# The last piece of a final RMS norm: a GpSimd power in place of ScalarE's inverse root and a Newton step

## The chip, the cores and the metric

The kernel runs on one core of a Trainium2 chip. The metric is the device time of one execution in microseconds (us); before the change the median of three runs is 1436.55 us (1436.22 to 1438.27).

## The reference

The kernel computes one layer of a streaming encoder on 1024 positions of 1024 channels: two convolution mixers with gates, an output projection, a SwiGLU feed-forward part, and at the end an RMS norm. Only the end is touched by the change:

```python
def rms_norm(x, g):
    xf = x.astype(jnp.float32)
    y = xf * lax.rsqrt(jnp.mean(xf * xf, axis=-1, keepdims=True) + EPS)
    return (y * g.astype(jnp.float32)).astype(x.dtype)

x = x + g2 * jnp.einsum('bsf,fd->bsd', jax.nn.silu(a) * bgate, w_ffn_out[l])
return rms_norm(x, final_norm_g)
```

For each position the square of 1024 channels is averaged, EPS = 1e-6 is added, and every channel of the position is multiplied by the inverse square root of the sum (called the factor here) and by its own gain g.

## The kernel before, in words

Channels lie on the 128 partitions, in eight tiles of 128 channels (j = 0 to 7); positions lie along a row of a tile. A factor for 256 positions is therefore a tile of 128 x 256 in which all partitions hold the same numbers: a product of TensorE with a matrix of ones sums over the partitions and writes the sum to each of them.

The last matrix products (the feed-forward part's second weights) are made with the positions cut in three pieces, `PIECES = [(0, 512), (512, 256), (768, 256)]`. For each piece and each j the evacuation from PSUM adds the product to x in place (L1994, VectorE). Then `piece_done` follows: ScalarE squares x with a scale of 1/32, so that the sum is a mean (L1967). For the tiles that GpSimd will scale, ScalarE also multiplies x by the gain (L1973). VectorE adds the squares up (L2017). When the piece has all its squares, `piece_norm` sums them over the partitions on TensorE (L2045, tile `ss` in PSUM), and ScalarE makes a first inverse root of `ss` with EPS as bias (L624, tile `rf`) and half its square (L2047, tile `rq`). `piece_rstd` improves it by a Newton step in two instructions of VectorE (L2054, L2056). They leave the negative of the factor, since the step is written as (t - 1.5) * r. The sign is undone by using `ng`, the negated gains, for the product with the gain.

`piece_scale` multiplies. Of the first two pieces GpSimd multiplies all eight tiles by the factor (L2033). Of the last piece, whose work comes after the last matrix product, GpSimd takes the tiles j = 1, 4 and 7 (`POOL_LAST`), and VectorE the other five, with gain and factor in one instruction (L2035). For this the last piece's factor is held twice: VectorE reads `rf` in PSUM, where the Newton step's second instruction writes it, and GpSimd reads `rp`, a copy in SBUF that ScalarE makes (L2024). SyncE's queue sends the results out as they come: the last two pieces in eight DMAs (L2038) of two tiles each, in the order of j. So the first DMA of the last piece waits for tile 0 of VectorE and tile 1 of GpSimd.

Each engine works through its own list in order, and waits for other engines at semaphores. The lists are set by the order of the code and by hints (`issue_after`); a scheduler places the instructions of the last pieces among those of the matrix products. Before the last piece's root a tiny ScalarE instruction with the same function (L650) is placed by `load_rsqrt`.

Of the kernel before, what the change touches and what calls it, by code (L numbers as in the profile page):

```python
# [35 lines left out]
F32 = mybir.dt.float32  # L36
F32R = mybir.dt.float32r
AF = mybir.ActivationFunctionType
ALU = mybir.AluOpType

P = 128
# [3 lines left out]
KC = D // P  # L45
# [8 lines left out]
V_GMIX, V_GFFN, V_GFIN, V_LNG, V_LNB, V_CB = (8 * i for i in range(6))  # L54
# [60 lines left out]
APART = 3  # L115
# [26 lines left out]
PIECES = [(0, 512), (512, 256), (768, 256)]  # L142
# [7 lines left out]
def block_kernel(ctx: ExitStack, tc: tile.TileContext, x0, xT, c, vecs, ada, w_first, w_plain, w_duals,  # L150
                 w_short, w_conf, w_o, w_fi, w_fo0, w_fo1, outT):
    nc = tc.nc

    def pool(name, bufs, **kw):
        return ctx.enter_context(tc.tile_pool(name=name, bufs=bufs, **kw))
# [10 lines left out]
    cp = pool("const", 1)  # L166
# [13 lines left out]
    def ps_tile(name):  # L180
        return psp.tile([P, H], F32, tag="ps", name=name)

    def ps2_tile(name):
        return ps2p.tile([P, H], F32, tag="ps2", name=name)

    def hl_tile(name, dt=F32R):
        return tp.tile([P, H], dt, tag="t", name=name)
# [7 lines left out]
    def f32(t):  # L195
        return t.bitcast(F32)
# [7 lines left out]
    vec = cp.tile([P, NV], F32, name="vec")  # L204
# [2 lines left out]
    nc.vector.memset(ones, 1.0)  # L207
    ones_c = cp.tile([P, P], F32R, name="ones_c")
    nc.gpsimd.memset(f32(ones_c), 1.0)
    eps1 = cp.tile([P, 1], F32, name="eps1")  # L210
    nc.vector.memset(eps1, EPS)
    eps2 = cp.tile([P, 1], F32, name="eps2")
# [4 lines left out]
    ng = cp.tile([P, V_LNG], F32, name="ng")  # L217
# [402 lines left out]
    def rstd_start(ss, eps, name, n=H, tile_of=g_tile):  # L620

        r, t = tile_of(name + "r")[:, :n], tile_of(name + "t")[:, :n]
        ss = ss[:, :n]
        act = nc.scalar.activation(r, ss, AF.Abs_reciprocal_sqrt, bias=eps)  # L624
        return ss, eps, r, t, act.ins
# [21 lines left out]
    def load_rsqrt(ins):  # L647

        with tc.issue_after(ins):
            act = nc.scalar.activation(cp.tile([P, 1], F32, name="rs"), ones[:, :1], AF.Abs_reciprocal_sqrt)  # L650
        load_rsqrt.ins = act.ins
# [94 lines left out]
    def uc_tile(name, n=T + CK - 1, dt=F32):  # L746
        return ucp.tile([P, T + CK - 1], dt, tag="uc", name=name)[:, :n]
# [30 lines left out]
    for k in range(0, KC, 2):  # L778
        t = uc_tile("x0", T)
# [477 lines left out]
    sqs = [None, None]  # L1257
# [565 lines left out]
    ss = ps_tile("ss")  # L1823
# [108 lines left out]
    for g in range(FINAL):  # L1932
        n = 2 * GROUPS[g] * P
# [20 lines left out]
    LAST = len(PIECES) - 1  # L1954

    def wide_tile(name):
        return hl_tile(name, dt=F32)

    def on_pool(i, j):
        return i < LAST or j in POOL_LAST  # L1960

    def piece_done(i, j):
        nonlocal norm, acc
        at, n = PIECES[i]
        dst = x1[j][:, at : at + n]
        sq = wide_tile("sq")[:, :n]
        act = nc.scalar.activation(sq, dst, AF.Square, scale=1.0 / 32.0)  # L1967
        sqs.append(sq)
        c = len(sqs) - 1
        if i == LAST and c == KC - 1:  # L1970
            load_rsqrt(act.ins)
        if on_pool(i, j):
            nc.scalar.activation(dst, dst, AF.Copy, scale=ng[:, V_GFIN + j : V_GFIN + j + 1])  # L1973
        lag = LAG if i == LAST else 0
        if c > lag and c - lag < KC - APART * (i == LAST):
            piece_sum(i, c - lag)
        if i and c == NORM_AT[i - 1]:
            norm = piece_norm(i - 1, [acc])
        if i and c == RSTD_AT:
            with tc.issue_after(last_evac.ins):  # L1980
                rf = piece_rstd(i - 1, *norm)
            piece_scale(i - 1, rf)
        if c == KC - 1 and i < LAST:
            acc = sqs[0]
            sqs.clear()

    def last_evac(d, i):
        at, n = PIECES[i]

        def evac(p, m, ps):  # L1990
            low = m in "574"
            j = 2 * d + p + 4 * low
            dst = x1[j][:, slice(at, at + n) if i else halves[m in "67"]]
            last_evac.ins = nc.vector.scalar_tensor_tensor(  # L1994
                out=dst, in0=ps, scalar=ng2[:, j : j + 1] if low else modc(40 + j), in1=dst, op0=ALU.mult, op1=ALU.add
            ).ins
            if m in "2453":
                piece_done(i, j)
        return evac

    def piece_product(banks, d, m, i):
        at, n = PIECES[i]
        off = at % H
        apart = (d, m) == (0, "5")
        for p in range(2):
            if m == "5":
                banks[d, p] = ps_tile("z")[:, :n]
            ps = banks[d, p]
            for k in range(KH):
                xs = tuple(t[:, off : off + n] for t in to[FINAL, m][k])  # L2010
                c0 = ((0 if apart else p) * KH + k) * P
                mm3([ps], slice(c0, c0 + P), w5[p] if apart else ws[d, m], [xs], m == "5" and k == 0, k == KH - 1, m == "3")
            last_evac(d, i)(p, m, ps)

    def piece_sum(i, j):
        with tc.issue_after(last_evac.ins):
            nc.vector.tensor_tensor(sqs[0], sqs[0], sqs[j], ALU.add)  # L2017

    def piece_scale(i, rf):
        at, n = PIECES[i]  # L2020
        m = H // n
        if i == LAST:
            rp = wide_tile("rp")[:, :n]
            nc.scalar.copy(rp, rf)  # L2024
        else:
            rp = rf
        for j in range(0, KC, m):
            ys = wide_tile("y") if m > 1 else x1[j][:, at : at + n]
            ys = ys.rearrange("p (m n) -> p m n", n=n)
            for d in range(m):  # L2030
                y, src = ys[:, d], x1[j + d][:, at : at + n]
                if on_pool(i, j + d):
                    nc.gpsimd.tensor_tensor(y, src, rp, ALU.mult)  # L2033
                else:
                    nc.vector.scalar_tensor_tensor(  # L2035
                        out=y, in0=src, scalar=ng[:, V_GFIN + j + d : V_GFIN + j + d + 1], in1=rf, op0=ALU.mult, op1=ALU.mult
                    )
            nc.sync.dma_start(outT[j : j + m, :, at : at + n].rearrange("m p n -> p m n"), ys)  # L2038

    def piece_norm(i, parts):  # L2040

        n = PIECES[i][1]
        ss, r, q = (t[:, :n] for t in (ps_tile("ss"), wide_tile("rf"), wide_tile("rq")))
        for part in parts:
            nc.tensor.matmul(ss, ones, part, start=part is parts[0], stop=part is parts[-1])  # L2045
        rstd_start(ss, eps1, "rf", n, lambda name: r)
        nc.scalar.activation(q, r, AF.Square, scale=0.5 ** 0.5)  # L2047
        return ss, r, q

    def piece_rstd(i, ss, r, q):  # L2050

        n = PIECES[i][1]
        t = ps2_tile("rft")[:, :n]
        nc.vector.scalar_tensor_tensor(out=t, in0=ss, scalar=EPS, in1=q, op0=ALU.add, op1=ALU.mult)  # L2054
        out = ps2_tile("rf")[:, :n] if i == LAST else r
        nc.vector.scalar_tensor_tensor(out=out, in0=t, scalar=1.5, in1=r, op0=ALU.subtract, op1=ALU.mult)  # L2056
        return out

    norm, acc, sqs = None, None, []
    for d in range(2):  # L2060
# [4 lines left out]
    for i in range(1, len(PIECES)):  # L2065
        banks = {}
        for m in "53":
            for d in range(2):
                if i == 1 and (d, m) != (0, "5"):
                    ws[d, m] = next_w()  # L2070
                piece_product(banks, d, m, i)
    piece_scale(LAST, piece_rstd(LAST, *piece_norm(LAST, [sqs[0]] + sqs[KC - APART :])))


def _chunks(v):
# [74 lines left out]
```

## Time and profile before

| | |
|---|---|
| median of three runs | 1436.55 us (1436.22 to 1438.27) |
| the profiled execution's own time | 1434.56 us |
| its span, first to last instruction | 1432.5 us |
| TensorE busy | 1419.0 us, 99% of the span |
| VectorE, ScalarE, GpSimd busy | 1201.2, 663.7, 538.6 us |
| last product of the last piece's sum (L2045) | runs from 1421.75 to 1423.64 us of the span |
| last DMA of results issued | at 1428.3 us |

The times in the timeline and the windows are microseconds from the span's start. TensorE is nearly always busy, so almost the whole span is its work; only the last nine microseconds, behind the last matrix product, belong to the other engines. That is where the change lies. A row of a timeline gives the start, the time that it covers, the engine, the line and operation, the tiles written and read, the shape, how many instructions are merged in the row, and in brackets how long the engine was idle before and what released it.

### The profile page before, as it was taken

To read this page: it belongs to the slowest core of one execution; us is meant where nothing else is said; L and a number is where in the kernel's file an instruction comes from. 1 tells how busy PE (TensorE), PEld (TensorE's weight loads), DVE (VectorE), ACT (ScalarE), POOL (GpSimd) and SP (SyncE) were. 2 spreads that over 40 slices of the span, in tenths; PEclk is the share of its full clock that TensorE was granted. 3 is DMA by queue.
4 is the path that set the end of the run, shared out by engine and by line. 5 is a ranking of instruction groups with operands and counts; after the bars stand their busy time and mean duration, and the time that the engine had idled before them with its cause. 6 is when DMAs were issued, how large, how long until landed. Compare 5 with 4: busy or idle time off the path is not lost.

```text
span 1432.5 us, 17797 instructions
## 1 busy us (share of the span) xinstructions
PE 1419.0 (99%) x6274; PEld 1165.3 (81%) x6274; DVE 1201.2 (84%) x1680; ACT 663.7 (46%) x980; POOL 538.6 (38%) x526
## 2 busy tenths in 40 slices
PE   9999999999999999999999999999999999999997
PEld 5888888888888888878888788888888888888887
DVE  8987998999998999989989987777867665866676
ACT  4873333333333446557454765444444433321235
POOL 0007877777677672012121211111111015653405
PEclk9999999999999999999999999999999999999999
DMA  9775654333337879978797667665454349996903
GB/s 365 273 234 161 192 191 147 103 118 104 124 116 223 225 227 337 261 221 175 229 282 225 164 189 245 211 205 176 155 176 156 127 149 342 385 379 196 348 1 118
DMA packets 103596, 295.50 MB, mean 206 GB/s; under 512 B 11682, under 2 KB 13730, under 8 KB 103507
## 3 DMA queue, kind: packets, MB, share of 16 engines
q1 hardware_dynamic: 51280, 161.50, 33.0%
q0 software_dynamic: 47040, 119.22, 29.9%
q10 hardware_dynamic: 5186, 13.64, 2.4%
q8 instruction: 49, 0.80, 0.2%
q14 instruction: 41, 0.33, 0.1%
HBM read 219.87 MB, written 84.41 MB: 212 GB/s over the span
## 4 chain that ended last, share of the span: by engine, by line
PE 90%; DVE 4%; ACT 1%; POOL 1%; issue 1%; DMA 1%; POOLq 0%; SPq 0%; DVEq 0%; ACTq 0%
PE bank L554 14%; PE bank L556 14%; PE bank L553 14%; PE x L556 8%; PE x L553 8%; PE x L554 8%; PE z L553 4%; PE z L556 4%; PE z L554 4%; PE y L553 2%; PE y L556 2%; PE y L554 2%; PE lead L549 1%; DVE wl L255 1%; POOL x L2033 1%
## 5 line engine op out<-in xcount | busy, mean ns | idle before, releaser
L254 ACT CAST wh<-raw 128x1024 fp32r<-128x1024 f32 (+2 forms) x256 | 265.0, 1037 | 379.1 <-PE bank L554 117.9
L255 DVE TENSOR_TENSOR wl<-raw,wh 128x1024 fp32r<-128x1024 f32 (+2 forms) x178 | 212.8, 1196 | 45.6 <-ACT wh L254 43.7
L255 POOL TENSOR_TENSOR wl<-raw,wh 128x1024 fp32r<-128x1024 f32 x78 | 195.6, 2520 | 71.9 <-ACT wh L254 71.7
L1212 DVE SCALAR_TENSOR_TENSOR c<-diff,vec,c 128x512 f32<-128x512 f32 x232 | 163.4, 748 | 1.5
L1781 POOL DMA_DIRECT2D hid<-stage x70 | 37.4, 534 | 312.5 <-DVE stage L610 301.7
L556 PE MATMUL bank<-th,wl 128*128 128x512 f32 x336 | 130.8, 389 | 0.0
L554 PE MATMUL bank<-tl,wh 128*128 128x512 f32 x336 | 130.7, 389 | 0.0
L553 PE MATMUL bank<-th,wh 128*128 128x512 f32 x336 | 130.7, 389 | 0.0
L556 PEld LDWEIGHTS bank<-th,wl 128*128 128x128 f32 x336 | 63.1, 188 | 13.3 <-POOL wl L255 0.3
L554 PEld LDWEIGHTS bank<-tl,wh 128*128 128x128 f32 x336 | 63.1, 188 | 13.1
L553 PEld LDWEIGHTS bank<-th,wh 128*128 128x128 f32 x336 | 63.1, 188 | 13.0
L553 PE MATMUL x<-th,wh 128*128 128x512 f32 x176 | 68.5, 389 | 0.0
L554 PE MATMUL x<-tl,wh 128*128 128x512 f32 x176 | 68.5, 389 | 0.0
L556 PE MATMUL x<-th,wl 128*128 128x512 f32 x176 | 68.4, 390 | 0.0
L1212 DVE SCALAR_TENSOR_TENSOR c<-u,wsum,c 128x512 f32<-128x512 f32 x96 | 66.8, 749 | 0.8
L610 DVE TENSOR_TENSOR stage<-g,stage 128x512 fp32r<-128x512 f32 x60 | 41.1, 688 | 24.0 <-ACT stage L609 24.0
L609 ACT CAST stage<-g 128x512 fp32r<-128x512 f32 x60 | 37.2, 620 | 51.8 <-DMA hid<-stage 34.9
L1805 POOL DMA_DIRECT2D th<-hid x77 | 41.2, 535 | 50.2 <-PE x L556 23.2
L1805 POOL DMA_DIRECT2D tl<-hid x77 | 41.2, 535 | 19.6 <-DMA tl<-hid 3.8
L553 PE MATMUL bank<-t2h,wh 128*128 128x512 f32 x112 | 43.6, 389 | 0.0
L554 PE MATMUL bank<-t2l,wh 128*128 128x512 f32 x112 | 43.6, 389 | 0.0
L556 PE MATMUL bank<-t2h,wl 128*128 128x512 f32 x112 | 43.6, 389 | 0.0
(794 smaller groups left out, 4117.6 us busy)
## 6 DMA issues: line engine op xcount, KB each, us to landing
hid<-stage POOLq DMA_DIRECT2D x70, 512.0 KB, 4.5
raw<-in_w_duals SPq DMA_DIRECT2D x65, 512.0 KB, 4.5
raw<-in_w_fi SPq DMA_DIRECT2D x45, 512.0 KB, 3.8
th<-hid POOLq DMA_DIRECT2D x77, 256.0 KB, 6.4
tl<-hid POOLq DMA_DIRECT2D x77, 256.0 KB, 6.2
ada<-in_ada SPq DMA_DIRECT2D x34, 512.0 KB, 5.4
raw<-in_w_fo SPq DMA_DIRECT2D x16, 512.0 KB, 6.4
raw<-in_ada SPq DMA_DIRECT2D x14, 512.0 KB, 3.6
```

Of the source, the lines that this page charges most:

```text
L254: hi = nc.scalar.copy(wh, raw)
L255: lo = lo_engine.tensor_tensor(wl, raw, f32(wh), ALU.subtract)
L549: mm3.ins = nc.tensor.matmul(ps, w[0][:, wsl], x, start=first, stop=last, skip_group_check=again).ins
L553: nc.tensor.matmul(ps, wh, xh, start=first, stop=False, skip_group_check=again)
L554: nc.tensor.matmul(ps, wh, xl, start=False, stop=False, skip_group_check=again)
L556: mm3.ins = nc.tensor.matmul(ps, wl, xh, start=False, stop=last, skip_group_check=again).ins
L609: t_split.act = nc.scalar.copy(hi, src).ins
L610: t_split.ins = nc.vector.tensor_tensor(lo, src, f32(hi), ALU.subtract).ins
L1212: tap.ins = nc.vector.scalar_tensor_tensor(out=out, in0=src[:, s : s + H], scalar=wt, in1=acc, op0=ALU.mult, op1=ALU.add).ins
L1781: nc.gpsimd.dma_start(hid_dram[key], s)
L1805: nc.gpsimd.dma_start(t, hid_dram[key][:, s])
L2033: nc.gpsimd.tensor_tensor(y, src, rp, ALU.mult)
```

## The change

A tile `power` of 128 x 256 is added that holds -0.5 everywhere; GpSimd fills it at the start. For the last piece alone, `piece_norm` now copies the mean square plus EPS from PSUM to SBUF on ScalarE (function Identity with EPS as bias, into `rf`), and GpSimd raises each element of it to the power in `power`, in place. `piece_rstd` is not called for this piece, and the tiny ScalarE instruction ahead of its root goes. The factor now is in SBUF first, where GpSimd reads it; ScalarE copies it to PSUM for VectorE. The factor is positive, so the last piece uses the gains `vec` and not the negated `ng`.

```diff
+    power = cp.tile([P, PIECES[-1][1]], F32, name="power")
+    nc.gpsimd.memset(power, -0.5)
...
-        if i == LAST and c == KC - 1:
-            load_rsqrt(act.ins)
         if on_pool(i, j):
-            nc.scalar.activation(dst, dst, AF.Copy, scale=ng[:, V_GFIN + j : V_GFIN + j + 1])
+            nc.scalar.activation(dst, dst, AF.Copy, scale=(vec if i == LAST else ng)[:, V_GFIN + j : V_GFIN + j + 1])
...
         if i == LAST:
-            rp = wide_tile("rp")[:, :n]
-            nc.scalar.copy(rp, rf)
+            rp, rf = rf, ps2_tile("rf")[:, :n]
+            nc.scalar.copy(rf, rp)
...
-                        out=y, in0=src, scalar=ng[:, V_GFIN + j + d : V_GFIN + j + d + 1], in1=rf, op0=ALU.mult, op1=ALU.mult
+                        out=y, in0=src, scalar=vec[:, V_GFIN + j + d : V_GFIN + j + d + 1], in1=rf, op0=ALU.mult, op1=ALU.mult
...
             nc.tensor.matmul(ss, ones, part, start=part is parts[0], stop=part is parts[-1])
+        if i == LAST:
+            nc.scalar.activation(r, ss, AF.Identity, bias=eps1)
+            nc.gpsimd.tensor_tensor(r, r, power, ALU.pow)
+            return r
         rstd_start(ss, eps1, "rf", n, lambda name: r)
...
-        out = ps2_tile("rf")[:, :n] if i == LAST else r
-        nc.vector.scalar_tensor_tensor(out=out, in0=t, scalar=1.5, in1=r, op0=ALU.subtract, op1=ALU.mult)
-        return out
+        nc.vector.scalar_tensor_tensor(out=r, in0=t, scalar=1.5, in1=r, op0=ALU.subtract, op1=ALU.mult)
+        return r
...
-    piece_scale(LAST, piece_rstd(LAST, *piece_norm(LAST, [sqs[0]] + sqs[KC - APART :])))
+    piece_scale(LAST, piece_norm(LAST, [sqs[0]] + sqs[KC - APART :]))
```

The lists of TensorE and SyncE are unchanged. Two more places on the lists matter. First the end of GpSimd's list, before the change: the two last tiles of the middle piece (read with `rf`), then the three tiles of the last piece (read with `rp`).

```order
L2033 TENSOR_TENSOR y<-x_10227,rf 128x256
L2033 TENSOR_TENSOR y<-x_10229,rf 128x256
L2033 TENSOR_TENSOR y<-x_9747,rp 128x256
L2033 TENSOR_TENSOR y<-x_9748,rp 128x256
L2033 TENSOR_TENSOR y<-x_10229,rp 128x256
```

And the same place with the change, where the waits at semaphores stand behind the rows:

```order
L2033 TENSOR_TENSOR y<-x_10229,rf 128x256 [waits PE_49]
L2033 TENSOR_TENSOR y<-x_10231,rf 128x256
L2048 TENSOR_TENSOR rf<-rf,power 128x256 [waits Activation_49]
L2033 TENSOR_TENSOR y<-x_9749,rf 128x256 [waits PE_49,Pool_49]
L2033 TENSOR_TENSOR y<-x_9750,rf 128x256 [waits DMASW2_49,PE_49]
L2033 TENSOR_TENSOR y<-x_10231,rf 128x256 [waits DMASW1_49,PE_49]
```

The power stands behind the whole middle piece and in front of the last piece's three tiles, the first of which waits for GpSimd's own semaphore (Pool_49).

Second the end of ScalarE's list, before the change: the last squares, then the small instruction (`rs`), the root, half its square and the copy.

```order
L1967 ACTIVATE sq<-x_9750 128x256
L1967 ACTIVATE sq<-x_10225 128x256
L650 ACTIVATE rs<-ones 128x1
L624 ACTIVATE rf<-ss,eps_101 128x256
L2047 ACTIVATE rq<-rf 128x256
L2024 COPY rp<-rf 128x256
```

With the change two instructions follow the squares, and the second waits for GpSimd:

```order
L1969 ACTIVATE sq<-x_9752 128x256 [waits DMASW3_49,DVE_49]
L1969 ACTIVATE sq<-x_10227 128x256 [waits DMASW6_49,DVE_49]
L2047 ACTIVATE rf<-ss,eps_103 128x256 [waits DMASW5_49,PE_49]
L2024 COPY rf<-rf 128x256 [waits Pool_49]
L2148 UNCONDITIONAL_BRANCH
```

On VectorE the two Newton instructions (L2054 and L2056) are gone from the end of the list; its five products (L2035) come straight behind the last evacuation, and now wait for ScalarE's copy.

## The prediction

> **What bounds the kernel now.** I read the page's first part, then the timeline of the last stretch, then the waits of SyncE's queue and the DMA share by windows.
>
> ```profile
> PE 1419.0 (99%) x6274; PEld 1165.3 (81%) x6274; DVE 1201.2 (84%) x1680; ACT 663.7 (46%) x980; POOL 538.6 (38%) x526
> ```
>
> TensorE sets the time up to its last product; no other engine's work counts there unless TensorE waits for it. Its list does not change. What the change can move is the tail, which the timeline shows whole:
>
> ```profile
> 1421.01 3.66 POOL L2033 TENSOR_TENSOR y<-x,rf 128x256 f32<-128x256 f32 x5
> ...
> 1421.75 1.89 PE L2045 MATMUL ss<-sq,ones 128*128 128x256 f32 x8
> ...
> 1423.67 0.47 ACT L624 ACTIVATE rf<-ss,eps 128x256 f32<-128x256 f32 x1 [0.70 <-PE ss L2045]
> 1424.18 0.42 ACT L2047 ACTIVATE rq<-rf 128x256 f32<-128x256 f32 x1
> 1424.63 0.43 DVE L2054 SCALAR_TENSOR_TENSOR rft<-ss,rq 128x256 f32<-128x256 f32 x1 [2.20 <-ACT rq L2047]
> 1425.09 0.43 DVE L2056 SCALAR_TENSOR_TENSOR rf<-rft,rf 128x256 f32<-128x256 f32 x1
> 1425.56 0.37 ACT L2024 COPY rp<-rf 128x256 f32<-128x256 f32 x1 [0.97 <-DVE rf L2056]
> 1425.96 2.05 DVE L2035 SCALAR_TENSOR_TENSOR y<-x,ng,rf 128x256 f32<-128x256 f32 x5 [0.44 <-ACT rp L2024]
> 1426.01 2.10 POOL L2033 TENSOR_TENSOR y<-x,rp 128x256 f32<-128x256 f32 x3 [1.34 <-ACT rp L2024]
> ```
>
> The chain is serial: sum, root, half square, two Newton instructions, copy, products. From the end of the sum (1421.75 + 1.89 = 1423.64) to the first product (1425.96) it takes 2.3 us. The first row matters as much: GpSimd is busy with the middle piece until 1421.01 + 3.66 = 1424.67 and idles 1.34 us before its own three tiles. Behind the products come the DMAs:
>
> ```profile
> SPq L2145 <- DMA outT<-y: 2.3, 2, 1.6
> SPq L2038 <- DVE y L2035: 1.8, 2, 1.4
> SPq L2038 <- POOL y L2033: 1.6, 3, 0.9
> ...
> outT<-y SPq DMA_DIRECT2D x4, 256.0 KB, 2.5
> ...
> 1426.60:1427.60 1.00, 0.00 (x0) 0.00 (x0) 1.00 (x4) 0.00 (x0) 1.00 (x3) 0.67 0.00 0
> 1427.60:1430.80 3.20, 0.00 (x0) 0.00 (x0) 0.41 (x2) 0.00 (x0) 0.51 (x1) 0.50 0.96 327
> ```
>
> SyncE's queue waits for the products, then for its DMAs. In the windows (the last two columns are DMA share and GB/s) the DMA engines are empty for 1.0 us and then full for 3.2 us: four DMAs at 0.8 us each. So the end is paced from the moment at which the first pair (tiles 0 and 1) is ready. Tile 0 is ready about 0.48 us after VectorE's start, 1426.44, and tile 1 at 1426.01 + 0.73 = 1426.74; GpSimd's decides.
>
> **The change part by part.** Removed from the tail: L624's root, L2047, L2054, L2056, in all from 1423.67 to 1425.52. The small instruction L650 ran while ScalarE waited for the sum, so taking it out gives nothing. Gains from `vec` or from `ng` are the same operand form: nothing.
>
> Added at the start is a MEMSET of 128 x 256 on GpSimd. These rows bound it and show what is behind it:
>
> ```profile
> L773 POOL MEMSET c<- 128x512 f32 x2 | 1.0, 530 | 0.0
> L773 POOL MEMSET first_row<- 128x128 f32 x1 | 0.2, 207 | 0.0
> ...
> 1.16 0.99 POOL L773 MEMSET c<- 128x512 f32 x2
> ...
> 2.24 0.71 POOL L775 DMA_DIRECT2D vec<-in_vecs  x1
> ...
> 2.69 1.13 ACT L786 ACTIVATE c<-diff 1x512 f32<-1x512 f32 x2
> ...
> 10.65 0.17 DVE L805 TENSOR_SCALAR ng<-vec 128x24 f32<-128x24 f32 x1
> ...
> vec<-in_vecs POOLq DMA_DIRECT2D x1, 184.0 KB, 6.2
> ```
>
> It lies between 0.2 and 0.53 us; I take 0.3 (between the two shapes). The zeroes of `c` are then there at 1.16 + 0.99 + 0.3 = 2.45, still ahead of ScalarE's first use at 2.69, which waits for its table. The load of `vec` lands near 2.24 + 0.3 + 6.2 = 8.7, two microseconds before VectorE reads it at 10.65. Cost nothing; without that cover it would be 0.3 us.
>
> Added in the tail: ScalarE's Identity with bias (nearest rows L624 at 0.47 and L2024 at 0.37, both reading PSUM at this shape), from 1423.67 to about 1424.14. GpSimd could begin then, but its middle piece holds it until 1424.67. So the Identity is hidden behind that piece, and the power begins at 1424.67. Let it take X. It ends at e = 1424.67 + X. Then ScalarE's copy to PSUM: 0.1 to hand over, 0.37 to run, 0.03 to VectorE (rows L2024 and L2035 above), so VectorE begins at e + 0.50 and has tile 0 at e + 0.98. GpSimd's tile 1 is ready at about e + 0.05 + 0.73 = e + 0.78, earlier. The first pair now hangs on VectorE, behind one copy more: e + 0.98 = 1425.65 + X against 1426.74 before. **The end moves by X - 1.1 us.** By the last pair instead (VectorE's five products at e + 0.50 + 2.05, against 1428.11) it is X - 0.9; I use the first, since the DMAs then run one behind another as before.
>
> What waits behind the power: on GpSimd the three tiles, on ScalarE only the copy, on VectorE all five products, and all four DMAs on SyncE. Nothing covers it.
>
> **The price of X.** The trace of before has no power. Rows that bound it:
>
> ```profile
> L2033 POOL TENSOR_TENSOR y<-x,rp 128x256 f32<-128x256 f32 x3 | 2.1, 728 | 1.3 <-ACT rp L2024 1.3
> L1201 POOL TENSOR_TENSOR diff<-u 128x15 f32<-128x15 f32 x8 | 2.4, 296 | 7.6 <-DVE u L1212 7.6
> L1243 POOL TENSOR_TENSOR tot<-tot,u 128x512 f32<-128x512 f32 x16 | 21.8, 1438 | 5.1 <-DVE u L1212 5.1
> ```
>
> Low end: the power is one pass like a product, with two inputs and one output, X = 0.73 (a gain of 0.4 us). GpSimd's time goes with the columns (728 ns for 256, 1438 for 512), so its price is one per column. A power is no single operation of arithmetic, though: worked as an exponential of a logarithm, with two series of eight terms, a multiplication and an addition for each, and a product between, it is 2 x 16 + 1 = 33 steps (my count, an assumption). High end: every step costs what a whole product of this shape costs, start to start (2.10 / 3 = 0.70): 33 x 0.70 = 23 us, a loss of 22 us. In between: a step inside the instruction reads nothing from memory and should be nearer to the cheapest pass, a fill, which takes 530 / 2 = 0.265 us for 256 columns. With all 33 steps 8.7 us, with half of them (multiplication and addition in one) 4.5. I take 25 steps, **X = 6.6 us**, nearest to the fill's row since the data stay inside. The end then moves by 6.6 - 1.1 = 5.5 us.
>
> [...]
>
> **The rivals.** *Cheap power*, X below 4: with steps packed many to a cycle, or few steps, the product's 0.73 us is the nearest row. At X = 1.6 the end moves by +0.5 us, no change that can be measured; X = 0.73 would give -0.4. For it: the product's own pass is dominated by moving data (columns, not operations, set the rows above), so arithmetic may fit into it. Against it: 33 steps in the room of a few. Faster than before it is below X = 1.1, and even X = 0 gains only 1.1 us. Time 1437.0.
>
> *First use.* The power may pay once more for being called for the first time. The trace has such a place:
>
> ```profile
> L329 POOL TENSOR_TENSOR raw<-raw x8: 2402/2412/3267, 107.0 to 145.8; 128x1024 f32<-128x1024 f32 x8
> L329 POOLq MODIFY_POOL_CONFIG  x2: 396/396/396, 85.1 to 85.2; - x2
> ```
>
> The slowest of GpSimd's first products took 3267 against 2412 ns, 0.86 us more, though other contention may be in it. A cheap power of 0.73 with that is X = 1.6, the number above. [...]
>
> *Serial power.* Each step waits for the one before and costs a whole pass, X = 23: the end moves by +22 us, time 1458.4. For it: one pass at 0.70 us has just one operation, and no row shows more of them in the same time. Against it: the passes contain reads and writes.
>
> That the change does nothing is excluded: the list of GpSimd has the power in the chain.
>
> **How the numbers follow.** The profiled execution took 1434.56 us for a span of 1432.5; adding 5.5 gives 1440.1 for it. The median of the runs stands 2.0 above, 1436.55, so the forecast for the median is 1436.55 + 5.5 = **1442.0**. A change of 0.2% is 2.9 us, about what a measurement of this kernel can tell from none; X - 1.1 = 2.9 puts that border at X = 4.0.
>
> Chances: dear power (X from 4 to 12) 0.42, time 1439.5 to 1447.5; cheap power, with or without a first use, 0.33; serial power (X over 12) 0.23; gain over 0.2% 0.02, which the bound at X = 0 leaves to a disturbance elsewhere. So faster 0.02, same 0.33, slower 0.65. The range reaches from the cheap end, 1436.55 - 0.4 and a bit for the spread of the runs, 1435.7, to just past the serial bound, 1460. The dear case's own range is 1439.5 to 1447.5.
>
> **What would show it.** Right: in the timeline after, one POOL row at L2048 of some 6.6 us from 1424.7 on, ScalarE's L2024 waiting for it, VectorE's five products 0.5 us behind its end, four DMAs full behind them; everything ahead of 1423.6 unchanged. Wrong: a POOL row below 4 us or above 12; a power that starts later than 1424.8; the first tile of GpSimd waiting much beyond 0.1 us behind it; a start of TensorE's first products that has moved.

## The result

The changed kernel takes 1477.7 us (median of four runs, 1476.17 to 1482.89) against 1436.64 us before (four runs, 1436.22 to 1438.27): 1.0281 times as long, 95% interval 1.0265 to 1.0297, some 41 us more. The forecast was 1442.0 us with a range up to 1460; the direction was right, the size far too small.

The tail of the changed kernel in the timeline (columns as before: start, time covered, engine, line, operation, tiles, and in brackets the idle time before and its releaser):

```profile
1423.94 3.65 POOL L2033 TENSOR_TENSOR y<-x,rf 128x256 f32<-128x256 f32 x5
1424.55 1.89 PE L2045 MATMUL ss<-sq,ones 128*128 128x256 f32 x8
...
1426.47 0.47 ACT L2047 ACTIVATE rf<-ss,eps 128x256 f32<-128x256 f32 x1 [0.79 <-PE ss L2045]
1427.55 41.27 POOL L2048 TENSOR_TENSOR rf<-rf,power 128x256 f32<-128x256 f32 x1
1468.85 0.38 ACT L2024 COPY rf<-rf 128x256 f32<-128x256 f32 x1 [41.90 <-POOL rf L2048]
1468.89 2.09 POOL L2033 TENSOR_TENSOR y<-x,rf 128x256 f32<-128x256 f32 x3
1469.25 2.05 DVE L2035 SCALAR_TENSOR_TENSOR y<-x,vec,rf 128x256 f32<-128x256 f32 x5 [44.02 <-ACT rf L2024]
```

One row holds the whole loss: L2048, the power, 41.27 us. ScalarE has idled 41.90 us when the copy begins, VectorE 44.02 us when its products begin. The windows of the same kernel, cut at the power's ends, show that no other engine computes meanwhile (busy time of PE, PEld, DVE, ACT and POOL, granted clock, DMA share, GB/s):

```profile
1427.50:1468.80 41.30, 0.00 (x0) 0.00 (x0) 0.00 (x0) 0.00 (x0) 41.30 (x2) 0.53 0.03 10
1468.80:1470.60 1.80, 0.00 (x0) 0.00 (x0) 1.35 (x4) 0.38 (x1) 1.72 (x4) 0.50 0.00 0
1470.60:1473.80 3.20, 0.00 (x0) 0.00 (x0) 0.70 (x2) 0.00 (x0) 0.38 (x1) 0.50 0.96 326
```

The 10 GB/s of the first window are the middle piece's last results; from 1429.5 us to the power's end the DMA engines are empty. The last piece's DMAs come behind as before, full for 3.2 us. From the end of the sum (1424.55 + 1.89 = 1426.44) to the end of the span (1475.8) it is 49.4 us; before it was 1432.5 - 1423.64 = 8.9. The tail is thus 40.5 us longer. In this profile the sum also ended 2.8 us later than in the one before; the fourth experiment below asks whether the change did that.

### The profile page after: what moved, and what is told of

The parts are those of the page before. It is cut to its first block, busy times and chain, and to the rows that moved or that the text cites. A ratio compares the mean times of both kernels' runs of the same rounds, so it can differ in the third digit from the quotient of the medians.

```text
span 1475.8 us, 17794 instructions
## 1 busy us (share of the span) xinstructions
PE 1419.5 (96%) x6274; PEld 1165.1 (79%) x6274; DVE 1200.4 (81%) x1678; ACT 662.9 (45%) x978; POOL 578.3 (39%) x528
## 4 chain that ended last, share of the span: by engine, by line
PE 82%; POOL 5%; DVE 4%; issue 3%; DMA 3%; ACT 2%; SPq 0%; DVEq 0%; POOLq 0%; ACTq 0%
PE bank L556 12%; PE bank L558 12%; PE bank L555 12%; PE x L558 8%; PE x L555 8%; PE x L556 8%; PE z L555 4%; PE z L558 4%; PE z L556 4%; POOL rf L2048 3%; PE y L555 2%; PE y L558 2%; PE y L556 2%; PE lead L551 1%; DMA raw<-in_w_short 1%
## 5 line engine op out<-in xcount | busy, mean ns | idle before, releaser
L612 DVE TENSOR_TENSOR stage<-g,stage 128x512 fp32r<-128x512 f32 x60 | 41.1, 687 | 24.4 <-ACT stage L611 24.3
L1807 POOL DMA_DIRECT2D tl<-hid x77 | 41.1, 533 | 24.0 <-DMA tl<-hid 6.2
```

What stands on the lines that cost most here:

```text
L612: t_split.ins = nc.vector.tensor_tensor(lo, src, f32(hi), ALU.subtract).ins
L1807: nc.gpsimd.dma_start(t, hid_dram[key][:, s])
```

## The experiments

Two questions were open: what the 41 us hang on (columns, elements, the first call, the numbers), and whether the rest of the change has a price of its own. In the diffs a minus line is of the changed kernel.

### Half the columns

```diff
-            nc.gpsimd.tensor_tensor(r, r, power, ALU.pow)
+            nc.gpsimd.tensor_tensor(r[:, : n // 2], r[:, : n // 2], power[:, : n // 2], ALU.pow)
```

> The power is raised on the first 128 of the 256 columns only; the other half of the factor stays the mean square, so that half of the result is left without its norm. In the changed kernel the power took 41.27 us. Theory A, a fixed price per column (41.27 / 256 = 161 ns): the power takes 20.6 us and the tail ends 20.6 us earlier than with the change. Theory B, one price for the first call (code that has to come in): it stays near 40 us, less at most 1 us. In between, the two points of 128 and 256 columns give the fixed part and the slope.

The row of the power's line in this kernel (count, then shortest, median and longest duration in ns, then first and last start):

```profile
L2048 POOL TENSOR_TENSOR rf<-rf,power x1: 20810/20810/20810, 1430.9 to 1430.9; 128x128 f32<-128x128 f32 x1
```

The time is 1460.52 us (one run). Half the columns take half the time. 128 columns fewer save 41.27 - 20.81 = 20.46 us, that is 160 ns for a column, and 20.81 - 20.46 = 0.35 us stand besides. Theory B falls for all but that 0.35 us. The time fell by 17.2 us and not by 20.5, since the sum ended 3.4 us later in this execution (1429.86); from the sum's end to the span's end it is 1458.7 - 1429.86 = 28.8 us against 49.4, 20.5 us less.

### Two calls, one behind the other

```diff
+            nc.gpsimd.tensor_tensor(q, r, power, ALU.pow)
             nc.gpsimd.tensor_tensor(r, r, power, ALU.pow)
```

> The same power is raised twice, one call behind the other on GpSimd, the first into a tile that nobody reads. Theory A (price per column): each call takes 41.3 us, 82.5 together, and the end moves by another 41.3 us. Theory B (first call alone is dear): the first takes about 41 us, the second 0.7 to 4 us, and the end moves by no more than 4 us.

GpSimd's timeline in this kernel:

```profile
1430.70 41.26 POOL L2048 TENSOR_TENSOR rq<-rf,power 128x256 f32<-128x256 f32 x1
1472.04 41.23 POOL L2049 TENSOR_TENSOR rf<-rf,power 128x256 f32<-128x256 f32 x1
```

The second call costs what the first does, 41.23 against 41.26 us, and the time is 1522.06 us (one run). A price for the first use is at most 0.03 us. The first call writes another tile and the second works in place, so that makes no difference beyond those 0.03 us either.

### One partition

```diff
-            nc.gpsimd.tensor_tensor(r, r, power, ALU.pow)
+            nc.gpsimd.tensor_tensor(r[:1], r[:1], power[:1], ALU.pow)
```

> The power is raised on one partition only, 256 columns; the factor of the other 127 partitions stays the mean square. If a column's price is the same however many partitions it holds (all lanes step together): 41 us as before. [...] Theory B: 40 us, as with the first, so this run speaks only on elements against columns.

```profile
L2048 POOL TENSOR_TENSOR rf<-rf,power x1: 41266/41266/41266, 1427.0 to 1427.0; 1x256 f32<-1x256 f32 x1
```

41.27 us for 256 numbers, as for 32,768 (1477.11 us, one run). The price is that of a column, full or not: by elements 41.27 / 128 = 0.32 us would have been left. How the engine works the partitions of a column off is not shown; of what was run, only fewer columns made the power shorter (20.81 us for 128).

### A product in the power's place

```diff
-            nc.gpsimd.tensor_tensor(r, r, power, ALU.pow)
+            nc.gpsimd.tensor_tensor(r, r, power, ALU.mult)
```

> The power is replaced by a product with the same tiles, so the factor is minus one half of the mean square and the result is not normed: it leaves the power out and keeps the rest of the change. By the sum of the prediction with X = 0.73 the end stands 0.4 us earlier than before the change, 1436.2 us for 1436.6, not to be told from no change (ratio 0.998 to 1.002). If the rest of the change costs something of its own (the wait behind the middle piece, the start, the 2.9 us by which the sum ended later in the profile of the changed kernel), it is 1439 us or more and the last product of the sum ends near 1426.5 instead of 1423.6.

The median is 1438.47 us, against 1438.93 us for the kernel before on the same chip; ratio 0.9993, interval 0.9977 to 1.0009. The rest of the change costs nothing that can be measured. Its tail:

```profile
1425.74 3.65 POOL L2033 TENSOR_TENSOR y<-x,rf 128x256 f32<-128x256 f32 x5
...
1426.45 1.89 PE L2045 MATMUL ss<-sq,ones 128*128 128x256 f32 x8
...
1428.38 0.47 ACT L2047 ACTIVATE rf<-ss,eps 128x256 f32<-128x256 f32 x1 [0.79 <-PE ss L2045]
1429.35 0.72 POOL L2048 TENSOR_TENSOR rf<-rf,power 128x256 f32<-128x256 f32 x1
1430.10 0.38 ACT L2024 COPY rf<-rf 128x256 f32<-128x256 f32 x1 [1.24 <-POOL rf L2048]
1430.14 2.09 POOL L2033 TENSOR_TENSOR y<-x,rf 128x256 f32<-128x256 f32 x3
1430.51 2.05 DVE L2035 SCALAR_TENSOR_TENSOR y<-x,vec,rf 128x256 f32<-128x256 f32 x5 [3.37 <-ACT rf L2024]
```

GpSimd reaches L2048 1.0 us behind the sum's end (1429.35 against 1428.34), held by the middle piece's last tiles, as forecast. VectorE begins 2.17 us behind the sum's end and has tile 0 at 2.65; before the change the first pair was ready at 3.10 (tile 1, 1426.74 - 1423.64). The gain to the first pair is 0.45 us, where the sum gave 0.4. From the sum's end to the span's end it is 1437.1 - 1428.34 = 8.8 us, against 8.9: most of the gain is lost again at the very end. The DMA engines are empty 6.7 us behind the sum's end, where it was 7.1 before, but the span's end follows 2.0 us later, where it was 1.7. A row of SyncE's waits for TensorE's sequencer (PEq) differs by as much (in all, times, longest), here and then before the change:

```profile
SPq L2148 <- PEq L2148: 1.0, 2, 0.8
SPq L2145 <- PEq L2145: 0.7, 2, 0.5
```

Why this wait is 0.3 us longer was not followed up. The changed kernel has it too (1.0, 2, 0.8).

Here too the sum ended later than in the profile of the kernel before (1428.34 against 1423.64), yet the time is the same as before. If the change delayed the sum by 2.8 us, the ratio here would be about 1.002, beyond the interval's upper end of 1.0009 (1.3 us). The sum's end lay between 1423.6 and 1429.9 in the ten profiles taken. The earliest is that of the kernel before, but its execution (1434.56 us) was faster than all 32 other runs of that kernel (1434.82 to 1444.0 us). So the 2.8 us are taken for the scatter of the long part ahead. They have arisen by the first DMA of the tile `th`, which starts at 854.4 us before the change and at 857.2 in the changed kernel. Which wait in that part varies was not followed up.

### Two columns

```diff
-            nc.gpsimd.tensor_tensor(r, r, power, ALU.pow)
+            nc.gpsimd.tensor_tensor(r[:, :2], r[:, :2], power[:, :2], ALU.pow)
```

> The power is raised on two of the 256 columns only (the other 254 keep the mean square, so nearly all of the result is left without its norm). The runs with 128 and 256 columns took 20.81 and 41.27 us: 160 ns for a column and 0.35 us besides. A straight line gives 0.35 + 2 x 0.16 = 0.67 us for two columns. If the instruction had a dearer fixed part that the line does not show, or worked on blocks of columns, it is above 1.5 us.

```profile
L2048 POOL TENSOR_TENSOR rf<-rf,power x1: 719/719/719, 1427.8 to 1427.8; 128x2 f32<-128x2 f32 x1
```

0.72 us against 0.67 by the line. The line holds down to two columns, with 0.40 us besides in place of 0.35 (1437.33 us, one run).

### Other exponents

```diff
-    nc.gpsimd.memset(power, -0.5)
+    nc.gpsimd.memset(power, 0.0)
```

> The exponent is 0 in place of minus one half, so every factor is 1 and the result is left without its norm; shape and code are those of the changed kernel. If the price of a column depends on the numbers (an early way out for an exponent of 0, branches on values), the power takes clearly less than 41 us. If the same steps run whatever the numbers are: 41.3 us, within 0.2.

```profile
L2048 POOL TENSOR_TENSOR rf<-rf,power x1: 41267/41267/41267, 1426.0 to 1426.0; 128x256 f32<-128x256 f32 x1
```

And with `nc.gpsimd.memset(power, 2.0)`:

> The exponent is 2, so the factor is the square of the mean square and the result is not normed. Same question with a whole exponent, which a power by repeated products would make in one or two steps: under 5 us by that way, 41.3 us within 0.2 if logarithm and exponential (or a fixed list of steps) run for every exponent.

```profile
L2048 POOL TENSOR_TENSOR rf<-rf,power x1: 41267/41267/41267, 1428.8 to 1428.8; 128x256 f32<-128x256 f32 x1
```

The exponent makes no difference beyond a nanosecond (41,266 ns with -0.5; times 1476.11 and 1478.96 us, one run each). No shorter time shows for 0 or 2; other bases were not tried.

### The factors laid on partitions

If a column costs 160 ns, full or not, the 256 factors belong into two columns of 128 partitions. `ident` is a unit matrix made at the start. Dots mark what is left out.

```diff
...
+            for b in range(m):
+                for part in parts:
+                    nc.tensor.matmul(ss[:, b : b + 1], part[:, blocks[b]], ones[:, :1], start=part is parts[0], stop=part is parts[-1])
...
-            nc.scalar.activation(r, ss, AF.Identity, bias=eps1)
-            nc.gpsimd.tensor_tensor(r, r, power, ALU.pow)
-            return r
+            nc.scalar.activation(r[:, :m], ss[:, :m], AF.Identity, bias=eps1)
+            nc.gpsimd.tensor_tensor(r[:, :m], r[:, :m], power, ALU.pow)
+            for b in range(m):
+                nc.vector.tensor_scalar(q[:, blocks[b]], ident, r[:, b : b + 1], None, ALU.mult)
+            rf = ps2_tile("rf")[:, :n]
+            nc.tensor.matmul(rf, ones, q, start=True, stop=True)
+            return rf
...
```

Here m = 2, `power` has two columns, and ScalarE copies `rf` from PSUM to `rp` for GpSimd as in the kernel before the change.

> The whole computation, with the 256 factors of the last piece laid on partitions: the sum over channels is made with the squares as weights and one column of ones, so that the mean square of 256 positions is a tile of 128 x 2; GpSimd raises two columns, VectorE spreads them on a diagonal, and one product with ones brings them back to 128 x 256. If the price is one of columns alone, the power takes 0.67 us and begins when GpSimd has done the middle piece, about 1.0 us behind the sum's end; with the diagonal (0.4), the product (0.5) and the copy (0.4) the factor is there about 0.9 us later than before the change. So: some 40 us faster than the changed kernel, and within 0.2% of the kernel before (ratio 1.000 to 1.002). If a one-time price or the tile's layout were the cause, it stays 30 us or more above the kernel before.

The median is 1440.73 us (11 runs), 1438.11 us for the kernel before on the same chip (15 runs): ratio 1.0012, interval 0.9998 to 1.0026. That holds what was expected, though the interval also allows a loss of 0.26%. The tail:

```profile
1424.89 1.27 PE L2051 MATMUL ss<-ones,sq 128*128 128x1 f32 x10 [0.46 <-ACT sq L1971]
1426.20 0.26 ACT L2052 ACTIVATE rf<-ss,eps 128x2 f32<-128x2 f32 x1 [1.37 <-PE ss L2051]
1426.57 0.72 POOL L2053 TENSOR_TENSOR rf<-rf,power 128x2 f32<-128x2 f32 x1
1427.33 0.48 DVE L2055 TENSOR_SCALAR rq<-ident,rf 128x128 f32<-128x128 f32 x2 [2.95 <-POOL rf L2053]
1427.87 0.71 PE L2057 MATMUL rf<-rq,ones 128*128 128x256 f32 x2 [1.71 <-DVE rq L2055]
1428.62 0.37 ACT L2026 COPY rp<-rf 128x256 f32<-128x256 f32 x1 [2.15 <-PE rf L2057]
1429.02 2.05 DVE L2037 SCALAR_TENSOR_TENSOR y<-x,vec,rf 128x256 f32<-128x256 f32 x5 [1.21 <-ACT rp L2026]
```

From the sum's end (1424.89 + 1.27 = 1426.16) to VectorE's first product it takes 2.86 us, 0.54 more than the root and the Newton step did (2.32); 0.9 was expected. The power began 0.41 us behind the sum's end and not 1.0. To the span's end it is 1436.0 - 1426.16 = 9.8 us against 8.9: of the 0.9 us more, 0.54 are these; where the other 0.4 arises was not followed up. It takes the 40 us back, but does not beat the kernel before; none of the kernels run does.

## Why the prediction was wrong

**The bound and the chain: right.** The tail is what the change moves. The power stands in the chain, begins behind the middle piece's tiles (1427.55, 1.1 us behind the sum's end; 1.03 forecast), and everything else of the last piece waits for it.

**The sum around X: right.** The end was to move by X - 1.1 us. With the measured X = 41.27 that is 40.2; the tail grew by 40.5 and the median of the runs by 1477.7 - 1436.64 = 41.1. The 0.3 us between 40.2 and 40.5 are as much as SyncE's longer wait at the very end, which the sum did not have. The hand-over from the power to VectorE took 1469.25 - 1468.82 = 0.43 us, where 0.50 was taken, and GpSimd's first tile begins 0.07 us behind the power. With a product in place of the power the first pair gained the forecast 0.4 us.

**The fill at the start and the tiny instruction: right.** In the changed kernel the fill took 0.32 us, where 0.3 was taken, and TensorE's first product and ScalarE's first use of `c` start where they did (1.61 and 2.70 us, before 1.62 and 2.69):

```profile
1.02 0.32 POOL L211 MEMSET power<- 128x256 f32 x1
```

With both edits in place and the power taken out, the ratio to the kernel before is 0.9993, interval 0.9977 to 1.0009.

**The price of X: the step that failed.** It was put at 6.6 us, 25 steps at the price of a fill, with a high end of 33 steps at the price of a whole product, 23 us. Measured is 41.27 us, 160 ns for a column: 59 whole products of 0.70 us, or 156 fills of 0.265 us where 25 were taken. That a step inside the instruction reads nothing from memory and costs about what a fill does, and that 25 of them make a power, was assumed, as was the cheap rival's ground, that moving data dominates a product's pass; no run shows any of these, only the whole price. The direction of the forecast, dearer than the border of 4 us, held; the size did not, and neither did the high end. That end was no bound: it joined a step count that was assumed, not read from any row, to a price for a step that no row showed either, and the top of the range, 1460, hung on it. Of the rivals the serial power was nearest (22 us, 0.23), and it too was short by nearly half. The cheap power, with 0.33, is excluded, as is the first use.

Why a column costs 160 ns is not shown. It does not hang on the partitions (41.27 us on 1 as on 128) or on the exponent (41.27 us for -0.5, 0 and 2), and not on the call's being the first (41.26 and 41.23 us).

## What to carry to other kernels

The same instruction with another operation can be dearer by a factor of 57 (41.27 against 0.72 us here): where the trace has no row for an operation, its price is unknown, and a bound from other operations' rows is none. A small run that costs the operation by itself comes ahead of putting it on a path that nothing covers. The power's price on GpSimd went by columns, full or not (41.27 us for 256 columns on 1 or 128 partitions, 0.72 us for two), so numbers that repeat over partitions belong on the partitions instead; and replacing 1.85 us of short instructions leaves little to win against even a moderate price.

## What was not expected of the hardware

GpSimd's elementwise power of 32-bit floats cost 160 ns for each column and 0.35 to 0.40 us besides, on 1 or 128 partitions, for the exponents -0.5, 0 and 2, the same from call to call within 0.03 us. ScalarE's Identity with a bias took 0.47 us on 128 x 256 from PSUM, exactly what its inverse root takes on the same tile: putting the one for the other saves nothing in itself. A copy took 0.37 us there.
